# Routed experts ordered by token count, with 64 slots for the three smallest

## The chip, the cores and the metric

The kernel runs on one core of a Trainium2 chip. The metric is the device time of one execution in microseconds (us). A whole network of thirteen stages is one program; the change touches only the twelfth, the routed experts.

## The reference

The stage computes, for 256 tokens `xt` of width 1024, eight experts of width 3584 and two experts per token:

```
logits = (xt @ w_router).astype(jnp.float32)
top_v, top_i = lax.top_k(logits, TOP_K)
gates = jax.nn.softmax(top_v, axis=-1)
comb = jnp.sum(jax.nn.one_hot(top_i, N_EXPERTS) * gates[..., None], axis=1)
y = jnp.zeros_like(xt)
for e in range(N_EXPERTS):
    y = y + comb[:, e:e + 1] * swiglu(xt, wg[e], wu[e], wd[e])
```

`swiglu(x, wg, wu, wd)` is `(silu(x @ wg) * (x @ wu)) @ wd`. `y` is added to the residual, and a last RMS norm follows. On the inputs of this case the reference's router gives the experts 0 to 7 these numbers of tokens: 58, 42, 99, 63, 66, 73, 32, 79 (512 in all, two for each token).

## The kernel before, in words

All arithmetic is float32, made of fp32r products: each operand is split into a high part (a cast to fp32r on ACT, `whi`, L462) and a low part (the rest, a subtraction on DVE, `wlo`, L463), and a product is the sum of three matmuls: high by high, low by high, high by low. `mm` (L326) issues every matmul.

The weights of an expert come as 42 tiles of 1 MB, 128 x 2048 (`load`, L431; the DMA is issued by SP at L435). An expert is cut into `NG` = 7 groups of 512 of its 3584 inner columns. A group takes two tiles of `moe_g`, two of `moe_u` and two of `moe_d`; every tile is converted in two halves of 128 x 1024. The raw tiles go round 13 buffers (`raw`, `raw2`, `raw3`), the converted halves round `W_BUFS` = 4 pairs of buffers. SP can issue a tile as soon as DVE has made the second low half of the tile 13 places ahead of it.

`moe_round` (L1875) runs the experts 0 to 7 in their order:

- `places(ep)` builds, for a pair of experts, the 0/1 matrices `pm` (token by slot, 128 slots an expert) and gathers the input of each by matmuls into `mpg`, split into `gh` and `gl`.
- `up(x, g)` is a group's gate and up product: the standing operand is `gh` or `gl` (128 slots), the moving one 512 columns of weights: 8 steps of 128 input features by 3 matmuls for each of `eg` and `eu`, 48 in all. Then `ea` = silu(`eg`) * `eu` (ACT L1935, DVE L1936).
- `turn` transposes `ea` in four 128 x 128 pieces into `ept` and splits it into `eah`, `eal` (L477, L478).
- `down(x, g)` adds the group to the expert's sums `eacc`: 4 pieces by 2 halves of the output by 3 matmuls, 24.
- `back` scales the sums by the gates (`eyh`, `eyl`, L1968 and L1969), scatters them to tokens with the transposed `pm` (`esc`) and adds them to `x` (L1975).

A group's `down` comes one group late, and `turn` stands between the gate and the up product of the next group; a scheduler then sets the order on each engine. After expert 0's first group, `rest()` computes the gates and the largest count. A second round follows if an expert has more than 128 tokens (L1857, L1858); with the counts above it is skipped.

Of the kernel before, what the change touches and what calls it, by code (L numbers as in the profile page):

```python
# [230 lines left out]
# ---------------------------------------------------------------- device program  # L231
# [14 lines left out]
def hybrid_stack_kernel(ctx: ExitStack, tc: tile.TileContext, A, out, voff, coff, stages=STAGES):  # L246
# [5 lines left out]
    # the tiles of the stages; before the routed experts they make room for more raw weights  # L252
# [60 lines left out]
    def g4(name, shape, dt=F32):  # L313
        return pools["attn" if "attn" in pools else "work"].tile(list(shape), dt, tag="g4", name=name, bufs=6)
# [38 lines left out]
    # constants used as they come, and those that are converted first  # L353
# [66 lines left out]
    # ---- weights  # L420
# [3 lines left out]
    def behind(insts):  # L424
        # keep what is traced inside from being issued before these
# [40 lines left out]
    def load_last(name, i):  # L466
        # in smaller steps, as nothing follows that could hide them
# [64 lines left out]
    def square_step(q, acc, m):  # L532
        # squares of the outputs as they end, and sums of the earlier ones
# [15 lines left out]
    class OutProj:  # L549
# [15 lines left out]
        def feed(self, hi, lo):  # L565
# [13 lines left out]
            if self.k == self.nk:  # L579
                # the two that come last lie in different banks  # L580
# [6 lines left out]
    # ---- norms  # L587
# [28 lines left out]
    def col_sums(o, parts, first=True, last=True):  # L616
        # sums over the partitions, one token per row: o [P, 2]
# [6 lines left out]
    def spread(o, c, start=False):  # L624
        # a value per token, from rows to every partition of o [., T]
# [214 lines left out]
    def stack_hl(rows, n, dst):  # L840
        # rows: psum [n, W] -> dst [64, W] with the two parts on rows 0.. and 32..
# [3 lines left out]
    # ---- state-space mixer  # L845
    def ssm_stage():
# [20 lines left out]
        # time steps  # L867
# [25 lines left out]
        # minus the running sums; the first chunk's also as seen from the second  # L893
# [107 lines left out]
    # ---- cross attention  # L1001
# [126 lines left out]
    # ---- gated MLPs  # L1128
# [51 lines left out]
    # ---- convolution module  # L1180
    def cf_stage():
# [7 lines left out]
        def gate(w, o):  # L1189
            for b in range(2):  # L1190
# [7 lines left out]
                # twice the gated value; the halves are taken back below  # L1198
# [3 lines left out]
        def taps_pe(n):  # L1202
            # some of the taps, as products with diagonal matrices
# [102 lines left out]
    def head_scale(tiles, nq, gq, gk, st):  # L1306
        # unit-norm heads in place; both gains and the scale go on the keys
# [92 lines left out]
    def run_heads(n, score, turn, out, fill=(), a=LEAD):  # L1400
        # three steps per head, each behind the next head's earlier ones
# [16 lines left out]
    def ab_stage():  # L1418
# [3 lines left out]
        for part in range(2):  # L1422
# [5 lines left out]
            if part == 0:  # L1428
                # forget gate: negative log and its running sum
# [39 lines left out]
            def bias(hd):  # L1469
                def f(p):  # L1470
# [3 lines left out]
                    # the running sums are of the negated logs  # L1474
# [20 lines left out]
    def cd_stage():  # L1495
        h = begin()
        # differential half
# [62 lines left out]
        # sliding window half: query tile t holds heads t and t + 4  # L1560
# [65 lines left out]
    # ---- gated convolution and linear recurrence  # L1626
    def hybrid_stage(l):
# [6 lines left out]
        # the gate comes as half of one plus a tanh  # L1634
# [46 lines left out]
        # recurrence  # L1681
        ybs = []
        ss, la_, bb = [], [], []
        for i in range(4):
# [7 lines left out]
            # 1 - a^2 = -tanh(log a) (1 + a^2)  # L1692
# [8 lines left out]
        for s in ss:  # L1701
            # the square root takes the quarter that is due to the halved gate
# [37 lines left out]
    # ---- routed experts  # L1740
# [13 lines left out]
    def route_step(j):  # L1754
        # the mean square and the router, from x as it comes
# [24 lines left out]
    def moe_stage():  # L1780
# [37 lines left out]
        # slots count from one; a token that is not routed has zero  # L1818
# [5 lines left out]
        # the token-major copy of the normalised input  # L1824
# [8 lines left out]
        def rest():  # L1833
            # exp of (v - max) for the two, over their sum
# [11 lines left out]
            cnt = keep.tile([P, 8], F32, name="cnt")  # L1846
            dve.tensor_copy(cnt, pr[:, 0, 16:24])
            mc = keep.tile([P, 1], F32, name="mc")
            dve.tensor_reduce(mc, cnt, axis=AX.X, op=OP.max)
# [3 lines left out]

        ci = []
        moe_round(0, hth, htl, sel, comb, lambda: ci.append(rest()))
        # an expert with more than 128 tokens takes a second round
        most = nc.values_load(ci[0][0:1, 0:1], min_val=0, max_val=T)  # L1857
        with tc.If(most > P):  # L1858
            dve.tensor_scalar(sel, sel, -float(P), 0.0, op0=OP.add, op1=OP.add)
            moe_round(1, hth, htl, sel, comb)  # L1860

    def xtok(t, n):
        # x by tokens, in the place of x by features
# [10 lines left out]
    # sums of squares for the last norm  # L1874
    ss = keep.tile([P, 2, 2], F32, name="ss")  # L1875

    def moe_round(rnd, hth, htl, sel, comb, rest=None):
        def places(ep):
            pm = [t1("pm", (P, 2, P), F32R) for _ in range(2)]
            for t in range(2):  # L1880
                for u in range(2):
                    e = 2 * ep + u
                    dve.tensor_scalar(pm[t][:, u, :], iota, sel[:, t, e : e + 1], 0.0, op0=OP.is_equal, op1=OP.add)
            # gathered inputs of the pair
            gh = [g4("gh", (P, KD, P), F32R) for _ in range(2)]
            gl = [g4("gl", (P, KD, P), F32R) for _ in range(2)]
            pgs = []
            for k2 in range(4):
                pg = ps("mpg")
                for j in range(2):  # L1890
                    k = 2 * k2 + j
                    cs = slice((k % 4) * P, (k % 4 + 1) * P)
                    for t in range(2):
                        r = pm[t].rearrange("p u s -> p (u s)")
                        mm(pg[:, j, :], hth[2 * t + k // 4][:, cs], r, j == 0 and t == 0, False)
                        mm(pg[:, j, :], htl[2 * t + k // 4][:, cs], r, False, j == 1 and t == 1)
                pgs.append(pg)
            for u in range(2):
                for k2 in range(4):
                    ks = slice(2 * k2, 2 * k2 + 2)  # L1900
                    split(pgs[k2][:, :, u * P : (u + 1) * P], gh[u][:, ks, :], gl[u][:, ks, :])
            return [(2 * ep + u, gh[u], gl[u], [None, None], pm, u) for u in range(2)]

        def places_back(x):
            # slot-major places, and gates by slot
            e, pm, u = x[0], x[4], x[5]
            pb = t1("pb", (P, T), F32R)
            pt = ps("mpt2")
            for t in range(2):
                pe.transpose(pt[:, 0, t * P : (t + 1) * P], f32v(pm[t][:, u, :]), ident)  # L1910
            for t in range(2):
                mm(pt[:, 1, :8], f32v(pm[t][:, u, :]), comb[:, t, :], False, t == 1)
# [3 lines left out]
            x[3][:] = [pb, g]  # L1916

        def up(x, g, mid):
            e, gh, gl = x[:3]
            po = [wv("eg"), wv("eu")]  # L1920
            po = [a.rearrange("p a b -> p (a b)") for a in po]
            for i, src in enumerate(("moe_g", "moe_u")):
# [164 lines left out]
```

## Time and profile before

| | |
|---|---|
| three runs | 2750.71, 2752.17, 2752.65 us; median 2752.17 |
| profiled execution | 2753.1 us, which is also its span |
| busy: PE, DVE, ACT | 2697.2, 2201.6, 1728.4 us |
| stage of the experts | about 1717 to 2740 us of the span |

The span is from the first to the last instruction. An engine's busy time is the sum of its instructions; matmuls overlap their neighbours and their ends are modelled, so what a matmul costs is the step from one start to the next in the timeline.

### The profile page before, as it was taken

The numbers are of one execution on the slowest core, as the hardware profiler recorded it, in microseconds if no ns is written. First come the engines' busy times: TensorE is split into PE (matmuls) and PEld (weight loads), VectorE is DVE, ScalarE is ACT, GpSimd is POOL, SyncE is SP. The second block draws the span as 40 slices with busy tenths as digits, with TensorE's granted clock in tenths as the row PEclk, the third lists the DMA queues.
The fourth block names the chain that finished last, engine by engine and source line by source line (L and its number), as shares of the span: only waits on it lengthen the run. The fifth ranks groups of instructions, "written<-read, shape, count | busy, mean of one in ns | idle before, by whom it ended". The sixth has DMA issues, their size and how long they took to land. (4 is left out here: it accounts for less than half of the span.)

```text
span 2753.1 us, 44558 instructions
## 1 busy us (share of the span) xinstructions
PE 2697.2 (98%) x17440; PEld 2398.0 (87%) x17440; DVE 2201.6 (80%) x3344; ACT 1728.4 (63%) x2563; POOL 7.7 (0%) x76
## 2 busy tenths in 40 slices
PE   8999999999999999999999999999999999999997
PEld 8799999999889988888999999888887878787876
DVE  8787597798668776767875577999998888888887
ACT  6665465565656555555654455877777777777776
POOL 0000000000000000000000000000000000000000
PEclk9999999999999999999999999999999999999999
DMA  7145445433435543342655554999999999999993
GB/s 260 62 169 184 138 155 189 162 108 123 169 117 190 184 145 127 113 139 100 260 198 184 184 177 169 347 363 351 351 343 343 339 349 359 349 344 343 362 343 115
DMA packets 87259, 620.05 MB, mean 225 GB/s; under 512 B 9936, under 2 KB 10064, under 8 KB 12800
## 3 DMA queue, kind: packets, MB, share of 16 engines
q1 hardware_dynamic: 86608, 616.57, 62.3%
q8 instruction: 138, 2.26, 0.3%
q14 instruction: 81, 0.66, 0.1%
q10 hardware_dynamic: 432, 0.56, 0.1%
HBM read 616.04 MB, written 1.05 MB: 224 GB/s over the span
## 5 line engine op out<-in xcount | busy, mean ns | idle before, releaser
L463 DVE TENSOR_TENSOR wlo<-raw,whi 128x1024 fp32r<-128x1024 f32 (+1 forms) x1164 | 1390.1, 1219 | 343.3 <-ACT whi L462 335.5
L462 ACT CAST whi<-raw 128x1024 fp32r<-128x1024 f32 (+1 forms) x1164 | 1195.6, 1049 | 573.8 <-PE wv L326 296.4
L326 PE MATMUL wv<-hh,whi 128*128 128x256 f32 x2400 | 681.2, 285 | 14.7 <-ACT hh L661 13.4
L326 PE MATMUL wv<-hl,whi 128*128 128x256 f32 x2400 | 680.1, 284 | 0.1
L326 PE MATMUL wv<-hh,wlo 128*128 128x256 f32 x2400 | 677.0, 283 | 1.6 <-DVE wlo L463 1.5
L326 PEld LDWEIGHTS wv<-hh,whi 128*128 128x128 f32 x2400 | 456.4, 190 | 18.7 <-ACT hh L661 14.6
L326 PEld LDWEIGHTS wv<-hh,wlo 128*128 128x128 f32 x2400 | 455.7, 190 | 4.1 <-DVE wlo L463 3.2
L326 PEld LDWEIGHTS wv<-hl,whi 128*128 128x128 f32 x2400 | 456.9, 190 | 1.8 <-DVE hl L662 0.7
L326 PE MATMUL eg<-wlo,gh 128*128 128x512 f32 x448 | 178.5, 398 | 2.8 <-DVE wlo L463 2.8
L326 PE MATMUL eu<-whi,gh 128*128 128x512 f32 x448 | 179.5, 401 | 0.0
L326 PE MATMUL eu<-wlo,gh 128*128 128x512 f32 x448 | 177.7, 397 | 1.4 <-DVE wlo L463 1.3
L326 PE MATMUL eg<-whi,gh 128*128 128x512 f32 x448 | 178.3, 398 | 0.0
L326 PE MATMUL eg<-whi,gl 128*128 128x512 f32 x448 | 177.2, 395 | 0.0
L326 PE MATMUL eacc<-whi,eal 128*128 128x512 f32 x448 | 177.1, 395 | 0.0
L326 PE MATMUL eacc<-whi,eah 128*128 128x512 f32 x448 | 177.0, 395 | 0.0
L326 PE MATMUL eu<-whi,gl 128*128 128x512 f32 x448 | 177.0, 395 | 0.0
L326 PE MATMUL eacc<-wlo,eah 128*128 128x512 f32 x448 | 162.6, 400 | 0.0
L326 PE MATMUL acc<-fl,whi 128*128 128x256 f32 x576 | 161.7, 281 | 0.0
L326 PE MATMUL acc<-fh,wlo 128*128 128x256 f32 x576 | 161.1, 280 | 0.0
L326 PE MATMUL acc<-fh,whi 128*128 128x256 f32 x576 | 160.6, 279 | 0.0
L837 DVE SCALAR_TENSOR_TENSOR cv<-pad,vec,cv 128x256 f32<-128x256 f32 x288 | 124.8, 479 | 1.4 <-ACT cv L834 0.6
L326 PEld LDWEIGHTS acc<-fl,whi 128*128 128x128 f32 x576 | 108.2, 188 | 0.3 <-DVE fl L478 0.3
(539 smaller groups left out, 4302.6 us busy)
## 6 DMA issues: line engine op xcount, KB each, us to landing
raw<-moe_u SPq DMA_DIRECT2D x112, 1024.0 KB, 7.1
raw<-moe_g SPq DMA_DIRECT2D x112, 1024.0 KB, 7.1
raw<-moe_d SPq DMA_DIRECT2D x111, 1024.0 KB, 7.0
raw<-ffn_in SPq DMA_DIRECT2D x44, 1024.0 KB, 5.0
raw<-sw_in SPq DMA_DIRECT2D x28, 1024.0 KB, 5.0
raw<-ffn_out SPq DMA_DIRECT2D x22, 1024.0 KB, 5.0
raw<-hy_in SPq DMA_DIRECT2D x20, 1024.0 KB, 5.0
raw<-ssm_in SPq DMA_DIRECT2D x18, 1024.0 KB, 5.2
```

Of the source, the lines that this page charges most:

```text
L326: return pe.matmul(o, l, r, start=start, stop=stop, skip_group_check=True)
L462: act.copy(hi[:, cs], raw[:, cs])
L463: dve.tensor_sub(lo[:, cs], raw[:, cs], f32v(hi[:, cs]))
L837: dve.scalar_tensor_tensor(y, pad[:, j, 4 - s : 4 + T - s], taps[i], y, op0=OP.mult, op1=OP.add)
```

## The change

It does four things. (1) The experts run in an order that is made on the chip: `rest()` sorts them by count (expert 0 stays first), writes the order to `idx`, and permutes slots, gates and counts (`selp`, `combp`, `cp`). SP loads each position's expert number from `idx` into a register and addresses the weights by it. (2) `RANKS` says which rank runs at which position, and `CAPS` how many slots it has: the ranks 5, 6 and 7 have 64, at the positions 2, 5 and 7. (3) For these, one operand `gx` of 128 columns holds the high part in 64 and the low part in 64, so that a product takes two matmuls. Rows 0 to 63 and 64 to 127 of the result are summed later: `turn_small` copies `eg` and `eu` out, and its products with `twice` (two identities of 64, one above the other) turn and sum at once; silu and the product with `eu` come after that, on 128 x 4 x 64. `down_small` again takes two matmuls. (4) Gathering is by the groups `GROUPS` (one or two experts). The second round starts if a count is above its position's slots.

```
+RANKS = [0, 1, 5, 2, 3, 6, 4, 7]
+SMALL = 64
+CAPS = [P if r < 5 else SMALL for r in RANKS]
+GROUPS = [[0], [1, 2], [3, 4], [5, 6], [7]]
...
 rest():
+            dve.scalar_tensor_tensor(key, cnt, 8.0, iota8, op0=OP.mult, op1=OP.subtract)
+            dve.tensor_scalar(key[:, 0:1], key[:, 0:1], 8.0 * T + 16.0, 0.0, op0=OP.add, op1=OP.add)
+            dve.max(out=kv, in_=key)
+            dve.max_index(ki, kv, key)
+            for j, r in enumerate(RANKS):
+                dve.tensor_scalar(oh[:, j, :], iota8, kf[:, r : r + 1], 0.0, op0=OP.is_equal, op1=OP.add)
+                dve.tensor_copy(idx[:, j : j + 1], kf[:, r : r + 1])
+            for src, dst in ((sel[:, 0], selp[:, 0]), (sel[:, 1], selp[:, 1]), (cnt, cp), (comb[:, 0], combp[:, 0]), (comb[:, 1], combp[:, 1])):
+                dve.tensor_tensor(tmp, oh, bc2(src, 8), op=OP.mult)
+                dve.tensor_reduce(dst, tmp, axis=AX.X, op=OP.add)
+            for j, c in enumerate(CAPS):
+                dve.tensor_scalar(cp[:, j : j + 1], cp[:, j : j + 1], float(T - c), 0.0, op0=OP.add, op1=OP.add)
-        with tc.If(most > P):
+        with tc.If(most > T):
...
+        def fetch(raw, src, e, i, cs=slice(0, 2048)):
+                    regs[e] = nc.values_load(
+                        route["idx"][0:1, e : e + 1], engines=[mybir.EngineType.SP], min_val=0, max_val=NE - 1
+                w = A[src][bass.ds(regs[e], 1), i : i + 1, :, cs].rearrange("a b p n -> (a b p) n")
...
 up():
-                        mm(po[i], gh[:, k, :], whi[:, cs], k == 0, False)
-                        mm(po[i], gl[:, k, :], whi[:, cs], False, False)
-                        mm(po[i], gh[:, k, :], wlo[:, cs], False, k == KD - 1)
+                        for a in gx:
+                            mm(po[i], a[:, k, :], whi[:, cs], k == 0 and a is gx[0], False)
+                        mm(po[i], gx[0][:, k, :], wlo[:, cs], False, k == KD - 1)
+                if not big:
+                    s.append(t2("es", (P, 512)))
+                    act.copy(s[i], po[i])
...
+        def turn_small(s):
+            pt = ps("ept", (P, 2, 4, SMALL))
+            for i in range(2):
+                for j in range(4):
+                    mm(pt[:, i, j, :], s[i][:, j * P : (j + 1) * P], route["twice"], i == 0 and j == 0, i == 1 and j == 3)
+            act.activation(a, pt[:, 0], AF.Silu)
+            dve.tensor_mul(a, a, pt[:, 1])
+            split(a, ax[:, :, :SMALL], ax[:, :, SMALL:])
...
+        def down_small(x, g, a, acc):
+                    for n in range(2):
+                        mm(acc[n], a[:, 2 * c + j, :], whi[:, cs], g == 0 and c == 0 and j == 0, False)
+                        mm(acc[n], a[:, 2 * c + j, :], wlo[:, cs], False, g == NG - 1 and c == 1 and j == 1)
```

The order of the instructions moves with it. Three places matter. The first is ACT in one group: before the change, in an ordinary group (`eah` belongs to the group ahead).

```order
L462 CAST whi_23192<-raw2_23190 128x1024
L462 CAST whi_23196<-raw2_23190 128x1024
L1935 ACTIVATE ea_23234<-eg_23135 128x512
L462 CAST whi_23214<-raw2_23212 128x1024
L462 CAST whi_23218<-raw2_23212 128x1024
L462 CAST whi_23239<-raw2_23237 128x1024
L462 CAST whi_23243<-raw2_23237 128x1024
L462 CAST whi_23261<-raw2_23259 128x1024
L462 CAST whi_23265<-raw2_23259 128x1024
L477 CAST eah_23332<-ept_23327 128x512
```

And with the change, on the same engine, in a group of the expert at position 2, the first with 64 slots.

```order
L470 CAST whi_22945<-raw2_22943 128x1024
L470 CAST whi_22949<-raw2_22943 128x1024
L2014 COPY es_22926<-eg_22888 128x512
L485 CAST eax_22940<-eas_22937 128x4x64
L470 CAST whi_22963<-raw2_22961 128x1024
L470 CAST whi_22967<-raw2_22961 128x1024
L470 CAST whi_22983<-raw2_22981 128x1024
L470 CAST whi_22987<-raw2_22981 128x1024
L2014 COPY es_22979<-eu_22889 128x512
L470 CAST whi_23001<-raw2_22999 128x1024
L470 CAST whi_23005<-raw2_22999 128x1024
L2037 ACTIVATE eas_23075<-ept_23066 128x256
```

Two instructions of 128 x 512 become two copies and two smaller ones, and each copy stands between two pairs of conversions. The second place is DVE where the stage starts, before the change: `sel` has just been made.

```order
L1883 TENSOR_SCALAR pm_20022<-direct_79,sel_20004 128x128 x2
L1883 TENSOR_SCALAR pm_20023<-direct_79,sel_20004 128x128 x2
L1849 TENSOR_REDUCE mc_20190<-cnt_20188 128x1
L1851 CAST ci_20192<-mc_20190 128x1
L1831 SCALAR_TENSOR_TENSOR mtl_20015<-mpx_19938,mSt_19964,mth_20014 128x512
L463 TENSOR_TENSOR wlo_20089<-raw3_20086,whi_20088 128x1024
```

With the change the same stretch of DVE reads as follows; 16 more instructions for `oh` and `idx`, ten for the permutations and eight for `cp` stand among the next eight conversions.

```order
L1951 TENSOR_SCALAR pm_20024<-direct_79,sel_20004 128x128
L1951 TENSOR_SCALAR pm_20025<-direct_79,sel_20004 128x128
L1861 SCALAR_TENSOR_TENSOR key_20182<-cnt_20180,direct_79 128x8
L1862 TENSOR_SCALAR key_20182<-key_20182 128x1
L1864 MAX kv_20185<-key_20182 128x8
L1866 MAX_INDEX ki_20187<-kv_20185,key_20182 128x8
L1868 CAST kf_20189<-ki_20187 128x8
L1839 SCALAR_TENSOR_TENSOR mtl_20015<-mpx_19938,mSt_19964,mth_20014 128x512
```

The chain of the sort stands ahead of `mtl`, the low part of the tokens that the gathering needs. The third place is SP with the change, at expert 0's fourth group.

```order
L1927 DMA raw3_20529<-moe_d 128x2048
L1927 DMA raw2_20553<-moe_g 128x2048
L1920 TENSOR_LOAD idx_20191
L1920 ISA x2
L1920 TENSOR_LOAD idx_20191
L1920 ISA x2
L1920 TENSOR_LOAD idx_20191
L1920 ISA x2
L1927 DMA raw2_20575<-moe_g 128x2048
```

Three loads of the order, which wait for DVE's `idx`, now stand ahead of the other 25 tiles of expert 0; from position 1 on, one register instruction (`ISA`) stands ahead of each DMA.

## Rows read from the trace of the kernel before

**Rows 1.** The page: busy time of each engine; 40 slices of DMA and GB/s.

```profile
PE 2697.2 (98%) x17440; PEld 2398.0 (87%) x17440; DVE 2201.6 (80%) x3344; ACT 1728.4 (63%) x2563; POOL 7.7 (0%) x76
...
DMA  7145445433435543342655554999999999999993
GB/s 260 62 169 184 138 155 189 162 108 123 169 117 190 184 145 127 113 139 100 260 198 184 184 177 169 347 363 351 351 343 343 339 349 359 349 344 343 362 343 115
```

**Rows 2.** Windows: busy PE, PEld, DVE, ACT, POOL; granted clock, DMA share, GB/s.

```profile
1751.62:1768.85 17.23, 17.23 (x78) 13.92 (x77) 15.74 (x16) 13.51 (x15) 0.00 (x0) 1.00 0.97 361
1768.85:1786.07 17.22, 17.22 (x78) 13.91 (x77) 15.72 (x15) 13.51 (x15) 0.00 (x0) 1.00 0.96 361
```

**Rows 3.** Timeline of PE: start, length, instruction, count.

```profile
2105.14 0.40 PE L326 MATMUL eu<-wlo,gh 128*128 128x512 f32 x1
2105.37 0.40 PE L326 MATMUL eu<-whi,gh 128*128 128x512 f32 x1
2105.60 0.40 PE L326 MATMUL eu<-whi,gl 128*128 128x512 f32 x1
...
1721.68 3.17 PE L326 MATMUL mpx<-mdg,xT 128*128 128x128 f32 x26
```

**Rows 4.** Timeline of DVE behind expert 3, and behind expert 2 (last two).

```profile
2253.11 6.89 DVE L463 TENSOR_TENSOR wlo<-raw,whi 128x1024 fp32r<-128x1024 f32 x6
2259.92 0.68 DVE L1936 TENSOR_TENSOR ea<-ea,eu 128x512 f32<-128x512 f32 x1
2260.52 6.96 DVE L463 TENSOR_TENSOR wlo<-raw,whi 128x1024 fp32r<-128x1024 f32 x6
...
2118.63 0.75 DVE L1969 SCALAR_TENSOR_TENSOR eyl<-eacc,gsl,eyh 128x512 fp32r<-128x512 f32 x1
2119.29 2.47 DVE L1975 TENSOR_TENSOR xT<-xT,esc 128x512 f32<-128x512 f32 x4
```

**Rows 5.** Groups of the stage, 1700 to 2750 us: count, busy us, mean ns, idle.

```profile
L462 ACT CAST whi<-raw 128x1024 fp32r<-128x1024 f32 x673 | 684.0, 1052 | 97.8 <-PE eg L326 39.9 <-PE eacc L326 30.6 <-PE eu L326 21.2
L477 ACT CAST eah<-ept 128x512 fp32r<-128x512 f32 x56 | 32.7, 585 | 71.2 <-PE ept L1942 71.2
L478 DVE TENSOR_TENSOR gl<-mpg,gh 128x256 fp32r<-128x256 f32 x32 | 12.7, 419 | 3.7 <-ACT gh L477 3.4
L477 ACT CAST gh<-mpg 128x256 fp32r<-128x256 f32 x32 | 11.2, 379 | 14.3 <-PE mpg L326 13.8 <-DVE gl L478 0.4
L1883 DVE TENSOR_SCALAR pm<-direct,sel 128x128 fp32r<-128x128 f32 x16 | 4.1, 280 | 0.0
```

**Rows 6.** Timeline of ACT: the first `eyh` of experts 3 to 6.

```profile
2244.39 0.69 ACT L1968 ACTIVATE eyh<-eacc,gsl 128x512 fp32r<-128x512 f32 x1 [3.38 <-PE eacc L326]
...
2369.19 0.69 ACT L1968 ACTIVATE eyh<-eacc,gsl 128x512 fp32r<-128x512 f32 x1 [3.38 <-PE eacc L326]
...
2497.77 0.69 ACT L1968 ACTIVATE eyh<-eacc,gsl 128x512 fp32r<-128x512 f32 x1 [3.38 <-PE eacc L326]
...
2622.60 0.69 ACT L1968 ACTIVATE eyh<-eacc,gsl 128x512 fp32r<-128x512 f32 x1 [3.38 <-PE eacc L326]
```

**Rows 7.** SP's waits, tiles landed, SP's timeline, its one register load.

```profile
SPq L435 <- DVE wlo L463: 801.4, 309, 6.6
...
raw<-moe_g SPq DMA_DIRECT2D x109, 1024.0 KB, 7.1
...
1758.10 2.79 SPq L435 DMA_DIRECT2D raw<-moe_g  x2
...
L1857 SPq TENSOR_LOAD <-ci x1: 481/481/481, 1731.6 to 1731.6; - x1
```

**Rows 8.** Timeline of DVE at the stage's start, in `rest()`.

```profile
1740.58 0.17 DVE L1842 TENSOR_TENSOR gt<-gt,gs 128x4 f32<-128x4 f32 x1
1740.78 0.17 DVE L1843 TENSOR_TENSOR o<-o,gt 128x16 f32<-128x16 f32 x1
1740.87 0.17 DVE L1844 TENSOR_TENSOR o<-o,gt 128x16 f32<-128x16 f32 x1
```

**Rows 9.** Windows elsewhere: columns as in rows 2.

```profile
15.00:20.00 5.00, 4.34 (x35) 3.93 (x34) 4.12 (x7) 3.23 (x4) 0.00 (x0) 1.00 1.03 420
340.00:344.00 4.00, 1.51 (x11) 1.38 (x11) 2.05 (x11) 2.99 (x5) 0.00 (x0) 0.91 0.18 76
344.00:348.00 4.00, 2.35 (x9) 1.76 (x9) 3.02 (x8) 1.79 (x4) 0.00 (x0) 0.50 0.00 0
748.00:752.00 4.00, 2.67 (x15) 2.04 (x15) 2.73 (x11) 3.99 (x14) 0.00 (x0) 1.00 0.56 231
```

More of the change, by code (lines that the diff above doesn't have):

```diff
@@ L313, in g4 @@
     def g4(name, shape, dt=F32):
-        return pools["attn" if "attn" in pools else "work"].tile(list(shape), dt, tag="g4", name=name, bufs=6)
+        if "attn" in pools:
+            return pools["attn"].tile(list(shape), dt, tag="g4", name=name, bufs=6)
+        return pools["work"].tile(list(shape), dt, tag="g4", name=name, bufs=5)
     def sm(name, shape, dt=F32):
@@ L1852, in rest @@
             return ci
+        selp = keep.tile([P, 2, 8], F32, name="selp")
+        combp = keep.tile([P, 2, 8], F32, name="combp")
         ci = []
-        moe_round(0, hth, htl, sel, comb, lambda: ci.append(rest()))
-        most = nc.values_load(ci[0][0:1, 0:1], min_val=0, max_val=T)
-        with tc.If(most > P):
-            dve.tensor_scalar(sel, sel, -float(P), 0.0, op0=OP.add, op1=OP.add)
-            moe_round(1, hth, htl, sel, comb)
+        moe_round(0, hth, htl, sel, selp, combp, lambda: ci.append(rest()))
+        most = nc.values_load(ci[0][0:1, 0:1], min_val=0, max_val=2 * T)
+        with tc.If(most > T):
+            for j, c in enumerate(CAPS):
+                dve.tensor_scalar(selp[:, :, j : j + 1], selp[:, :, j : j + 1], -float(c), 0.0, op0=OP.add, op1=OP.add)
+            moe_round(1, hth, htl, selp, selp, combp)
     def xtok(t, n):
@@ L1961, in down @@
                         mm(acc[n], ah[:, f], wlo[:, cs], False, g == NG - 1 and c == 1 and j == 1)
+        def down_small(x, g, a, acc):
+            e = x[0]
+            for c in range(2):
+                end = e == NE - 1 and g == NG - 1 and c == 1
+                wt = (load_e_last if end else load_e)("moe_d", e, 2 * g + c)
+                for j in range(2):
+                    whi, wlo = wt[j]
+                    for n in range(2):
+                        cs = slice(n * 512, (n + 1) * 512)
+                        mm(acc[n], a[:, 2 * c + j, :], whi[:, cs], g == 0 and c == 0 and j == 0, False)
+                        mm(acc[n], a[:, 2 * c + j, :], wlo[:, cs], False, g == NG - 1 and c == 1 and j == 1)
         def back(x, acc):
-            pb, gs = x[3]
+            pb, gs = x[2]
             yh = [t2("eyh", (P, 512), F32R) for _ in range(2)]
@@ L1977, in back, with step_down, turned @@
                         act.activation(t2("fsq", (P, 512)), xtok(t, n), AF.Square, accum_out=ss[:, t, n : n + 1])
-        todo = places(0)
+        def step_down(late):
+            x, g, a, acc = late
+            if acc is None:
+                acc = [ps("eacc", (P, 512)) for _ in range(2)]
+            (down if x[4] else down_small)(x, g, a, acc)
+            if g == NG - 1:
+                back(x, acc)
+                acc = None
+            return acc
+        def turned():
+            if late:
+                late[2] = (turn if late[0][4] else turn_small)(late[2])
+        todo = places(GROUPS[0])
         late = None
@@ L1990, in moe_round @@
                 if late is not None:
-                    y, gg, aa, ac = late
-                    if ac is None:
-                        ac = [ps("eacc", (P, 512)) for _ in range(2)]
-                    down(y, gg, aa, ac)
-                    acc = ac
-                    if gg == NG - 1:
-                        back(y, ac)
-                        acc = None
+                    acc = step_down(late)
                 late = [x, g, a, acc]
-                if g == 3 and e % 2 and e < NE - 1:
-                    todo += places((e + 1) // 2)
+                if g == 3 and not todo and e < NE - 1:
+                    todo += places(next(q for q in GROUPS if q[0] == e + 1))
                 if g == 4:
                     places_back(x)
-        y, gg, aa, ac = late
-        down(y, gg, turn(aa), ac)
-        back(y, ac)
+        turned()
+        step_down(late)
     def final_stage():
```

98 lines of the change are left out of this document (72 added, 26 removed).

## The prediction, made before the change was run

> **What bounds the kernel now.** I read the page first, then windows of the experts' stage, then the timelines of single engines. The page [rows 1] shows PE busy for 98% of the span, but in the last 16 of 40 slices, the experts, the DMA engines are also at nine tenths and DVE close behind; busy shares don't say which of the three gives the pace. The windows do. Two neighbouring groups of an expert [rows 2] last 17.22 us each, with PE busy throughout, DVE for 15.7, ACT for 13.5. In the timeline of PE a matmul of 512 columns starts 0.233 us after the one before [rows 3], whatever its listed length: 72 of them are 16.8 us, and four transposes fill the rest. So PE bounds a group. ACT waits for it: the conversion's idle time, 97.8 us in all, ends on PE [rows 5]. SP waits 801 us for DVE to give buffers back [rows 7], so weights are ahead of their use.
>
> How far ahead sets what happens when PE gets faster. A tile has 17.22 / 6 = 2.87 us; its buffer is issued anew 13 tiles ahead, 37.3 us; 7.1 us go until it lands [rows 7], some 3 us in conversion. About 27 us are left, or nine landed tiles.
>
> **What the change removes.** In a group of 64 slots `up` goes from 48 matmuls to 32, `down` from 24 to 16. That is 24 x 0.233 = 5.6 us of PE in each of 3 x 7 = 21 groups, 118 us in all. It would be the gain if PE stayed the bound. The sum over the other engines says that it doesn't.
>
> **A small group, engine by engine.** PE: 48 x 0.233 = 11.2 us, plus eight products with `twice`, 128 x 64 columns in full float32. The trace has no such shape. The nearest row, `mpx` [rows 3], gives 3.17 / 26 = 0.12 us for an instruction of 128 columns and two instructions to a product: 0.24 us as upper end, 0.12 with half the columns as lower. So 0.9 to 1.9 us, and PE needs 12.1 to 13.1.
>
> DVE: twelve low parts, and two operations on 128 x 256. Six low parts back to back take 2259.92 - 2253.11 = 6.81 us [rows 4], 1.135 each, so 13.6; the two are priced by `gl`, 0.42 each [rows 5], 14.5 us together. ACT: twelve casts, two copies like `eah`, 0.585 each, two like `gh`, 0.38 [rows 5]: at its full lengths 14.6 us, less for overlapped ends. So **DVE becomes the bound**, PE idles a sixth of the time, and what ACT makes DVE wait comes on top. The listed order of ACT in a small group has a copy of `eg`, later of `eu`, between conversions, and each waits for the last matmul of its product. From the end of the low part that this product needs last: four matmuls 0.93, copy 0.59, the cast of `eax` 0.38 (first point only), the next conversion 1.05 [rows 5], three handoffs of some 0.05: 3.1 and 2.7 us. DVE has two low parts (2.3), and at the first point `eax`'s 0.42, in hand. It idles about 0.4 us each time. A small group takes 14.5 + 0.8 = **15.3 us** in place of 17.22.
>
> **Experts.** Before, the distance between the scaled sums of neighbouring experts is 124.8, 128.6, 124.8 us [rows 6]; 128.6 is one that also gathers the next pair. I take 124.6 and 4.0 for a gathering, hidden by nothing since PE is full.
> - A small expert: 7 x 15.3 = 107.1. The expert ahead of it adds its `back` on DVE: two `eyl` 1.5 and four `xT` 2.5 [rows 4], 4.1 with `gsl`; and ACT's two waiting `eyh` delay conversions, for which I take 1.0 by the bubbles above (nothing to 3.4, the wait in [rows 6], are the ends). Together 112.2.
> - The one at position 2 gathers the pair 3 and 4 too. On DVE: four `gl` as before 1.7, four of half the width and four `pm` by the row of `pm`, 0.28 each: 2.2 [rows 5]. So 116.1.
> - Sum: 340.5 against 3 x 124.6 = 373.8: 33.3 gained.
> - Gatherings on PE in large experts: three before, 12.0; now at positions 0, 4 and 6, the last with 128 columns a matmul (2 to 4 us, take 3): 11.0. One more gained.
>
> **At the start** DVE gets 5 instructions of the sort and 16 for `oh` and `idx`, ten for the permutations, eight for `cp`, before PE has work ahead. A dependent small step is 0.20 us, an independent one 0.09 [rows 8]: 15 x 0.20 + 24 x 0.09 = 5.2 us. It loses four `gl` at some 0.36, since expert 0 is gathered alone, and a little of `pm`. Net 3.6 us, taken as fully on the path (nothing and 5.2 are the ends). **At the end** the last conversion is followed by 4 matmuls instead of 6, and PE no longer lags: 1 us gained.
>
> SP's three loads of the order, 0.48 us each [rows 7], wait for `idx`, which stands behind seven conversions in DVE's order, about 8 us at 1.135 each and the small steps; 25 tiles of expert 0 stand behind them. Nine landed tiles cover that. If they were gone, a few us would show. A register step per DMA is nothing against 2.87 us per tile.
>
> Sum: 33.3 + 1.0 - 3.6 + 1.0 = 31.7 us off 2753.1, so 2721. The profiled execution is 0.9 us above the median of the runs: **2720 us**.
>
> **Do the weights keep up?** A small expert uses 42 tiles in 112 us, 2.67 us each. In [rows 2] the engines moved 361 GB/s, 2.90 us a tile of 1.049 MB, and that was demand, not a limit: [rows 9] has 420. At 361, a small expert draws 42 - 112 / 2.90 = 3.4 tiles from the nine, a large one adds 0.9. After position 2 that leaves 5.6, 7.5 ahead of position 5, 4.1 behind it, 5.0 ahead of position 7, and 1.6 at the end. So the stock lasts even then.
>
> The Trainium skill's page DMA: Bandwidth & Descriptors, section Where 436 GB/s comes from, puts a limit of about 358 GB/s from HBM for each core, and by it a group's six tiles would need 17.6 us, so that without a stock nothing could be gained. The trace disagrees in short windows (420 GB/s), and its longest stretch near full, the last slices of [rows 1], has 363 at most, which was demand.
>
> **The rivals.**
> - *DMA takes over.* For it: a share of 0.97 in [rows 2]. Against: SP waits for buffers, and the stock above. If the stock were nothing and 361 a limit, a small group would take 17.4 us, and only `back`, gatherings and the end remain: about 2746. With a stock used up halfway, 2733.
> - *ACT gives the pace.* If its copies and waits don't overlap, or the eight joining products hold up PE's queue, on which `eu`'s matmuls stand behind them, a group takes 16.2 us: 19 us more, 2739.
> - *Only DVE's work counts*: no bubbles, 14.5 us a group, 17 us less: 2703.
> - *Slower: the clock.* PE idles a sixth of the time in small groups. Where PE had done little, at 340 us (busy 1.5 of 4), the granted clock fell to 0.50, the lower of the two levels, 1.2 GHz [rows 9]. At twice the step a small group's PE takes 25 us, 21 x 8 = 168 us above now: about 2920. It decides from a share of a good third of half-rate time (12.6 x 1.37 = 17.2). Against: gaps of tenths of a us, and a clock of 1.00 where PE was busy 2.67 of 4 us [rows 9]. The skill's page TensorE: Matmul & The Clock Gate, section What's actually happening, says that the clock is halved after idleness and returns with activity; [rows 9] agree.
> - *Slower: a second round*, if the change doesn't do what it says: a count above 64 at a small position would repeat the stage, some 970 us. The counts sorted, expert 0 apart, are 99, 79, 73, 66, 63, 42, 32; the largest of the last three is 63. It takes 65. A register-addressed DMA that needed over 2.9 us to issue would also be slower, by what it exceeds.
>
> **How the numbers follow.** DVE's pace with its bubbles, 2710 to 2732: 0.65. Work alone, down to 2700: 0.10. ACT's pace: 0.10. DMA partly or wholly: 0.08, of it 0.02 at no change. Clock 0.04; a second round or slow DMAs 0.02; nothing for a reason not seen 0.01. The range, 2702 to 2741, has the bounds of a group's price (14.5 to 16.2) and of the start; it leaves out the lost stock, the clock and the rest. A measurement here tells 0.2%, 5.5 us, from no change: faster 0.91, same 0.03, slower 0.06.
>
> **What would show it.** Small experts lasting 110 to 118 us, with PE's clock at 1.00, DVE busy in over nine tenths of them and PE waiting for `wlo`; large experts as before; SP still waiting for DVE. It is wrong if `wlo` or `whi` waits for DMA in a small expert, if ACT's waits for `eg`, `eu` and `ept` exceed 2 us a group, if PE's steps there are above 0.233 us, or if the start costs over 6 us.

## The result, and the profile after

The changed kernel takes 2700.51 us (median of four, 2699.77 to 2704.30) against 2752.01 for the kernel before (four): a ratio of 0.9817, 95% interval 0.9803 to 0.9831. Faster, as forecast, but by 51.5 us instead of 32, and 1.5 us below the low end of the range.

The page of the changed kernel, the three lines that answer to [rows 1]:

```profile
PE 2630.7 (97%) x17220; PEld 2319.6 (86%) x17220; DVE 2189.1 (81%) x3385; ACT 1733.5 (64%) x2605; POOL 7.7 (0%) x76
...
DMA  7145345533535543343655555799999999999993
GB/s 265 63 158 200 134 153 192 179 110 107 175 109 184 188 145 125 126 156 102 250 189 188 187 178 184 259 340 355 364 373 393 351 347 340 359 408 369 341 377 154
```

PE loses 66.5 us of work; six slices rise to 364 to 408 GB/s: the three small experts. Windows of two neighbouring small groups (columns as in [rows 2]):

```profile
2401.76:2416.92 15.16, 14.62 (x65) 10.29 (x64) 14.47 (x16) 13.22 (x17) 0.00 (x0) 1.00 1.01 407
2416.92:2432.08 15.16, 14.61 (x65) 10.29 (x64) 14.47 (x16) 13.22 (x17) 0.00 (x0) 1.00 1.01 414
```

A group takes 15.16 us with DVE busy for 14.47, where the forecast had 15.3 and 14.5. Of the listed time of PE, 14.6, some 2 us are waiting inside matmuls: its 48 steps of 0.233 us and the 16 instructions of the turning, 0.091 us each, need 12.6. What a group takes beyond DVE's work are two gaps in the timeline of DVE, here one group:

```profile
2408.62 2.36 DVE L471 TENSOR_TENSOR wlo<-raw,whi 128x1024 fp32r<-128x1024 f32 x2 [0.36 <-ACT whi L470]
2410.90 0.41 DVE L2038 TENSOR_TENSOR eas<-eas,ept 128x256 f32<-128x256 f32 x1
2411.23 6.89 DVE L471 TENSOR_TENSOR wlo<-raw,whi 128x1024 fp32r<-128x1024 f32 x6
2418.04 0.42 DVE L486 TENSOR_TENSOR eax<-eas,eax 128x256 fp32r<-128x256 f32 x1
2418.79 4.63 DVE L471 TENSOR_TENSOR wlo<-raw,whi 128x1024 fp32r<-128x1024 f32 x4 [0.33 <-ACT whi L470]
```

They come where the forecast put them, 0.33 and 0.36 us instead of 0.4, and behind ACT's waits for PE at the copies, in the timeline of ACT:

```profile
2407.06 0.59 ACT L2014 COPY es<-eu 128x512 f32<-128x512 f32 x1 [0.61 <-PE eu L334]
2407.54 2.00 ACT L470 CAST whi<-raw 128x1024 fp32r<-128x1024 f32 x2
2409.76 0.38 ACT L2037 ACTIVATE eas<-ept 128x256 f32<-128x256 f32 x1 [0.23 <-PE ept L334]
2410.05 5.78 ACT L470 CAST whi<-raw 128x1024 fp32r<-128x1024 f32 x6
2416.92 0.59 ACT L2014 COPY es<-eg 128x512 f32<-128x512 f32 x1 [1.09 <-PE eg L334]
```

So the group went as forecast. (The three waits shown are 1.9 us a group, just under the 2 us that the prediction named as a sign of being wrong.) The surprise stands elsewhere. The stage's first DVE operation behind the mean square, `rvs`, and the first `eal`, the low part of expert 0's first group, in the timeline of DVE before the change, and then after it:

```profile
1719.80 0.16 DVE L611 TENSOR_SCALAR rvs<-ms 128x2 f32<-128x2 f32 x1 [3.25 <-PE ms L326]
...
1751.62 0.69 DVE L478 TENSOR_TENSOR eal<-ept,eah 128x512 fp32r<-128x512 f32 x1
```

```profile
1706.99 0.16 DVE L619 TENSOR_SCALAR rvs<-ms 128x2 f32<-128x2 f32 x1 [3.26 <-PE ms L334]
...
1743.78 0.68 DVE L486 TENSOR_TENSOR eal<-ept,eah 128x512 fp32r<-128x512 f32 x1
```

**12.8 us are won before the stage starts**, in eleven stages whose instructions and order are the same, but for one of 0.21 us on DVE that makes `twice`, at 17.8 us. From `rvs` to the first `eal` the change is 5.0 us slower (36.79 against 31.82), from there to the end 42.8 us faster (958.7 against 1001.5).

Two things differ ahead of the stage. The first is the clock. A window of the kernel before, and the same work after:

```profile
1282.00:1292.20 10.20, 10.20 (x41) 6.10 (x39) 5.07 (x23) 5.67 (x23) 0.00 (x0) 0.50 0.08 31
```

```profile
1276.45:1282.15 5.70, 5.70 (x41) 3.70 (x39) 5.02 (x23) 4.61 (x20) 0.00 (x0) 1.00 0.14 56
```

The profiled execution before ran 10.2 us at the lower level there, 1.2 GHz, the one after did not; what takes 10.2 us there takes 5.7 after, so that the distance of the two grows by 4.5 us at that place. The second is slow growth everywhere: 95 consecutive starts of `wv` products with 256 columns, in the timeline of PE. Second and last of them, before:

```profile
289.02 0.28 PE L326 MATMUL wv<-hl,whi 128*128 128x256 f32 x1
...
300.18 0.28 PE L326 MATMUL wv<-hh,wlo 128*128 128x256 f32 x1
```

And the same two after:

```profile
287.71 0.28 PE L334 MATMUL wv<-hl,whi 128*128 128x256 f32 x1
...
298.68 0.28 PE L334 MATMUL wv<-hh,wlo 128*128 128x256 f32 x1
```

94 steps take 11.16 us and 10.97: 118.7 ns and 116.7 a step. Over 6,300 such pairs of neighbours in each trace the means are 118.2 and 116.8: some 8.5 us of PE's time, against the 8.3 us that the clock leaves of the 12.8.

### The profile page after: what moved, and what is told of

It reads as the page before. It is cut to its first block, busy times and chain, and to the rows that moved or that the text cites. A ratio compares the mean times of both kernels' runs of the same rounds, so it can differ in the third digit from the quotient of the medians.

```text
span 2702.4 us, 44795 instructions
## 1 busy us (share of the span) xinstructions
PE 2630.7 (97%) x17220; PEld 2319.6 (86%) x17220; DVE 2189.1 (81%) x3385; ACT 1733.5 (64%) x2605; POOL 7.7 (0%) x76
## 5 line engine op out<-in xcount | busy, mean ns | idle before, releaser
L334 PEld LDWEIGHTS wv<-hh,whi 128*128 128x128 f32 x2400 | 456.5, 191 | 17.6 <-ACT hh L669 13.8
L334 PE MATMUL eu<-whi,gx 128*128 128x512 f32 x728 | 245.7, 400 | 0.0
L334 PE MATMUL eg<-whi,gx 128*128 128x512 f32 x728 | 245.0, 398 | 0.0
L334 PE MATMUL eg<-wlo,gx 128*128 128x512 f32 x448 | 184.8, 412 | 10.2 <-DVE wlo L471 9.9
L334 PE MATMUL eu<-wlo,gx 128*128 128x512 f32 x448 | 185.0, 413 | 5.0 <-DVE wlo L471 4.2
L334 PEld LDWEIGHTS eg<-whi,gx 128*128 128x128 f32 x728 | 137.0, 190 | 29.6 <-ACT whi L470 0.6
L334 PEld LDWEIGHTS eu<-whi,gx 128*128 128x128 f32 x728 | 135.3, 188 | 27.2 <-ACT whi L470 0.9
L334 PEld LDWEIGHTS eg<-wlo,gx 128*128 128x128 f32 x448 | 84.5, 189 | 51.8 <-DVE wlo L471 34.5
L845 DVE SCALAR_TENSOR_TENSOR cv<-pad,vec,cv 128x256 f32<-128x256 f32 x288 | 124.7, 478 | 1.4 <-ACT cv L842 0.6
L334 PEld LDWEIGHTS eu<-wlo,gx 128*128 128x128 f32 x448 | 84.1, 188 | 40.2 <-DVE wlo L471 23.3
L334 PE MATMUL eacc<-whi,eah 128*128 128x512 f32 x280 | 110.5, 395 | 0.0
L334 PE MATMUL eacc<-whi,eal 128*128 128x512 f32 x280 | 110.5, 395 | 0.0
```

What stands on the lines that cost most here:

```text
L334: return pe.matmul(o, l, r, start=start, stop=stop, skip_group_check=True)
L845: dve.scalar_tensor_tensor(y, pad[:, j, 4 - s : 4 + T - s], taps[i], y, op0=OP.mult, op1=OP.add)
```

## The experiments

Besides that one instruction, what the change does to those stages is in memory. `keep`, the pool of what lasts, grew by 384 bytes a partition (`twice`, `selp`, `combp`, `idx`, less `cnt`). The pool behind it, with all raw and converted weights, begins that much later: the first `whi` at byte 63040 of its partition instead of 62656, by the addresses in the two built programs.

**The place alone.** The kernel before, with 384 unused bytes (in the experts 16 instead of 20 small buffers make room):

```
+        gap = keep.tile([P, 96], F32, name="gap")
+        pool.memset(gap, 0.0)
```

> The kernel before, with nothing of the change but 384 unused bytes per partition ahead of the pool of raw and converted weights, so that this pool lies where the changed kernel has it. Theory A (12.8 us of the gain come ahead of the experts, from the place of the converted weights in SBUF): 2739 to 2746 us, the 256-column product step near 116.9 ns instead of 118.2, and the first DVE rvs near 1707 to 1713 us instead of 1719.8. Rival B (those 12.8 us belong to the run or the chip, not to the program): 2751 to 2753 us, step 118.2 ns.

Measured: 2744.24 us against 2751.09, ratio 0.9974 (0.9963 to 0.9986); `rvs` at 1708.02. The same two matmuls:

```profile
288.16 0.28 PE L326 MATMUL wv<-hl,whi 128*128 128x256 f32 x1
...
299.13 0.28 PE L326 MATMUL wv<-hh,wlo 128*128 128x256 f32 x1
```

10.97 us again. The place of a pool is worth 6.9 us, 0.26%, with not one instruction of the experts changed. In its profile 11.8 us are won by `rvs`, since this execution too lacks the stretch at 1282 us. And the other way round, the change with its tables in the experts' own pool:

```
-            tw = route["twice"] = keep.tile([P, SMALL], F32, name="twice")
+            tw = route["twice"] = early("twice", [P, SMALL])
...
-        selp = keep.tile([P, 2, 8], F32, name="selp")
-        combp = keep.tile([P, 2, 8], F32, name="combp")
+        selp = early("selp", [P, 2, 8])
+        combp = early("combp", [P, 2, 8])
```

> The changed kernel, with its three new kept tables (384 bytes) moved into the experts' own pool, so that the pool of weights lies where the kernel before has it. Theory A: 2707 to 2713 us, first rvs back near 1714 to 1720 us, step 118.2 ns. Rival B: 2699 to 2702 us, step 116.9 ns.

Measured: 2710.38 us (0.9848, 0.9835 to 0.9862), mean step 118.5 ns. Theory A stands in both directions.

**The small slots alone.** The change with 128 slots everywhere (`CAPS = [P for r in RANKS]`, six buffers for `gx`, 16 small buffers):

> The changed kernel with 128 slots for all eight experts: sorting, loads by register and the new gatherings stay, the 64-slot path is gone. If the three small experts are worth 14 us each, and the rest of the change costs some 5 us at the start of the stage while 12.8 us are won ahead of it: 2742 to 2748 us. Rival (the order by count and the single gatherings bring a good part of the gain in the experts): under 2738 us. Rival (the 64-slot path brings all of it, and the 12.8 us belong to the run): over 2751 us.

Measured: 2751.07 us, 0.9997 (0.9988 to 1.0006). The first expectation was too low by 3 us, and the last one right in number, but half of its reason is wrong: the 12.8 us don't belong to the run. The four profiled spans give a chain: before 2753.1, moved pool 2742.1, all large 2751.2, the change 2702.4. From the moved pool to all large: 0.4 us ahead of `rvs`, 5.0 from `rvs` to `eal`, 3.7 behind it, where the positions 0 and 7 are now gathered alone, so that the stage pays for five gatherings instead of four (position 6, which now gathers for 7, takes 128.8 us instead of 124.9). From all large to the change: 48.8 us, of which 47.3 behind `eal` and 1.5 ahead of `rvs`, where the two programs do the same.

**The start.** First the order of the experts written into the program, with no sort and no register:

```
+ORDER = [0, 2, 3, 7, 5, 1, 4, 6]
...
-                w = A[src][bass.ds(regs[e], 1), i : i + 1, :, cs].rearrange("a b p n -> (a b p) n")
+            w = A[src][ORDER[e], i][:, cs]
```

> The changed kernel with the order of the experts written into the program (the order that these inputs give): no sorting on VectorE, no number of an expert in a register, plain addresses in all loads of expert weights; the 64-slot path stays. If the sorting behind the second product of expert 0 costs the 5 us by which the stage's start became longer: 2695 to 2697.5 us, and from the first rvs to the first eal 32 us instead of 36.8. Rival (the start is longer by the two single gatherings or by the halved clock there): 2699 to 2702 us. Rival (loads by register hold up SP's queue all along): under 2692 us.

Measured: 2705.08 us; `rvs` to `eal` 36.57. The sort costs 0.2 us, not 5, and loads by register cost nothing that can be seen. Windows of the change show what the start loses:

```profile
1708.10:1711.50 3.40, 3.40 (x17) 3.15 (x16) 2.30 (x19) 0.15 (x1) 0.00 (x0) 0.50 0.96 349
1711.50:1718.30 6.80, 4.82 (x44) 4.46 (x43) 5.76 (x19) 6.59 (x11) 0.00 (x0) 1.00 0.85 328
1718.30:1725.10 6.80, 6.80 (x23) 5.93 (x24) 6.08 (x18) 3.79 (x8) 0.00 (x0) 0.50 0.71 251
```

10.2 us at half the clock are worth 5.1. Was that chance? The change once more:

> The changed kernel itself, once more beside the kernel before. If the two short halvings of the granted clock at the start of the experts' stage (1708 to 1711 and 1718 to 1725 us in its first profile) came by the chance of that execution: most executions at 2699 to 2702 us with a mean granted clock of 0.993, single ones near 2704 us with 0.991. If they belong to the program: all near 2704 us, as in the kernel with the order written in (2705.1 us at 0.990 to 0.991).

Measured: 2705.34 us, five executions from 2701.35 (mean granted clock 0.993) to 2705.89 (0.990), ratio 0.9823 (0.9809 to 0.9836). By the mean clock some executions of the change have these stretches, and others hardly any. Then two kernels whose first gathering is 256 columns wide as before: the fixed order in four pairs, `GROUPS = [[0, 1], [2, 3], [4, 5], [6, 7]]`, and the change itself with expert 0's places twice, the second half unused:

> The kernel with the order of the experts written in, gathered in four pairs as in the kernel before instead of one, three pairs, one. Against the fixed order in groups of one, two, two, two, one (2705.1 us): theory (five gatherings cost the 5 us that the all-large kernel lost against the moved kernel before inside the experts): 2699 to 2702 us. Rival (the number of gatherings costs nothing, the halved clock at the start is all): 2704 to 2706 us, or with the halvings gone 2700 to 2701 us and the steps within the experts as they were.

> The changed kernel with the first gathering 256 columns wide, expert 0's places twice, the second half unused, so that TensorE does at the start of the experts' stage what it did before the change. Theory (the halved clock at the start comes with the products of 128 columns, and is the whole loss there): no stretch at 0.5 between 1690 and 2690 us, first rvs to first eal 32 to 33 us instead of 36.8, 2699 to 2701 us, each execution at a mean of 0.992 to 0.993. Rival (the start is longer since one expert alone is gathered, or by the place of the clock's windows): 35 us or more, 2703 to 2706 us.

```
-            w = len(es) * P
+            w = T if es[0] == 0 else len(es) * P
...
+                if es[0] == 0:
+                    dve.tensor_copy(pm[t][:, P:], f32v(pm[t][:, :P]))
```

Measured: 2698.60 and 2700.16 us, clock 0.992 or 0.993 in all eight executions, `rvs` to `eal` 31.88 and 31.77. Windows of the wide one:

```profile
1707.10:1710.50 3.40, 3.40 (x29) 3.26 (x30) 2.86 (x21) 1.45 (x3) 0.00 (x0) 1.00 0.98 330
...
1717.30:1724.10 6.80, 6.80 (x33) 5.58 (x32) 6.77 (x8) 5.69 (x9) 0.00 (x0) 1.00 0.81 267
```

With the clock up the start costs nothing, sort and all. Of the profiles here, the six kernels that gather 256 columns first have no stretch at 0.50 in the start; all that gather 128 have one or two. But the earlier one begins 1.1 us behind `rvs`, some 6 us ahead of the first gathering, where PE's order is the same in both. So how the width comes to matter stays open. The pairs take 1.6 us less: they have one gathering less, and no sort.

**What bounds a small group.** The product `eas * ept` left out (the output lacks that factor for the small experts):

```
-            dve.tensor_mul(a, a, pt[:, 1])
```

> The changed kernel without the product of the silu with the up half in the 64-slot groups (0.4 us of VectorE and one hand-over in each of 21 groups; the output lacks that factor for these experts). Theory (VectorE's work and its two short waits set the 15.15 us of such a group): 14.65 to 14.8 us in the steady groups, 2691 to 2695 us. Rival A (the weights' transfers at 411 GB/s set it): 15.15 us, 2699 to 2702 us. Rival B (the chain through ScalarE's copies sets it): 15.1 us or more, 2698 us or more.

Measured: 15.04 us a group, 2703.64 us. DVE has 0.33 us less to do and gets 0.11 back. Its timeline:

```profile
2403.11 0.42 DVE L486 TENSOR_TENSOR eax<-eas,eax 128x256 fp32r<-128x256 f32 x1
2403.86 4.63 DVE L471 TENSOR_TENSOR wlo<-raw,whi 128x1024 fp32r<-128x1024 f32 x4 [0.33 <-ACT whi L470]
2408.85 8.26 DVE L471 TENSOR_TENSOR wlo<-raw,whi 128x1024 fp32r<-128x1024 f32 x7 [0.35 <-ACT whi L470]
```

Where the product stood, the next low part now waits inside its group of seven (8.26 us against 7 x 1.135 + 0.08 = 8.03): ACT's chain, which waits at each copy, is only 0.1 us behind DVE. The time is rival B's: nothing is gained on the change. So the copies were put off by one weight tile, to when their products have ended:

```
-                    act.copy(s[i], po[i])
+                    held.append([2, s[i], po[i]])
...
+            while held and held[0][0] == 0:
+                with behind([raws["cast"]]):
+                    act.copy(*held.pop(0)[1:])
```

> The changed kernel with ScalarE's copies es of the 64-slot groups issued one weight tile later (two casts each), when their products have ended. Theory (VectorE's two waits of 0.4 us a group are ScalarE standing at es for TensorE, 1.0 and 0.6 us, before the next cast): steady groups 14.5 to 14.9 us instead of 15.15, 2688 to 2698 us with the change itself at 2700 to 2705. Rival A (the four buffers of converted halves make ScalarE wait for TensorE anyhow, at the cast instead of the copy): 15.0 to 15.15 us. Rival B (the transfers, 6.29 MB a group, end at 411 to 418 GB/s): 15.05 us or more.

Measured: 14.93 us a group, 2705.56 us. Timeline of ACT, and then of DVE:

```profile
2407.35 0.38 ACT L2043 ACTIVATE eas<-ept 128x256 f32<-128x256 f32 x1 [1.84 <-PE ept L334]
```

```profile
2407.77 0.42 DVE L2044 TENSOR_TENSOR eas<-eas,ept 128x256 f32<-128x256 f32 x1
2408.71 2.36 DVE L471 TENSOR_TENSOR wlo<-raw,whi 128x1024 fp32r<-128x1024 f32 x2 [0.52 <-ACT whi L470]
2410.99 0.42 DVE L486 TENSOR_TENSOR eax<-eas,eax 128x256 fp32r<-128x256 f32 x1
2411.32 11.44 DVE L471 TENSOR_TENSOR wlo<-raw,whi 128x1024 fp32r<-128x1024 f32 x10
```

Both waits at the copies are gone; one came back, at the joined product `ept`, which now comes later. The steady groups gain 0.22 us each, but the kernel isn't faster than the change. From the first `ea` of position 1 to that of position 3 this profile takes 230.5 us instead of 232.3, and from 4 to 6 238.8 instead of 239.5. Behind the first `ea` of position 6 it loses 4.8: there it has a stretch of 6.8 us at 0.50, at 2677 us near the end of the last small expert, that the change doesn't have. That stretch is worth 3.4 at most; where the rest goes was not followed up. With a fifth pair of buffers in the experts as well, for one raw buffer less:

> As the kernel with the late copies, with a fifth pair of buffers for converted halves in the experts, in the place of one of 13 buffers for raw weights. Theory (the loop of four buffers between ScalarE, VectorE and TensorE sets what VectorE still waits): VectorE without waits, 14.45 to 14.6 us a group, 2685 to 2692 us, at 432 to 435 GB/s. Rival (the transfers set the pace): 15.0 us or more a group at 411 to 420 GB/s, 2698 us or more. Rival (VectorE's waits were the late copies alone): no gain over the kernel with the late copies.

Measured: 14.93 us again, 2707.25 us. The loop of four buffers is not what DVE waits for. The transfers aren't either: [rows 2] had 361 GB/s, the groups above 407 and 414, and SP still waits for DVE to give buffers back, 36.6 of the 45 us from 2395 to 2440 us of the change. Its waits there:

```profile
SPq L1927 <- DVE wlo L471: 24.0, 12, 2.5
SPq L1927 <- DVE eas L2038: 6.5, 3, 2.5
SPq L1927 <- DVE eax L486: 6.1, 3, 2.0
```

The Trainium skill's page DMA: Bandwidth & Descriptors, section Where 436 GB/s comes from, has about 358 GB/s from HBM as a core's limit; these windows pass it by some 15%. The Trainium skill's page Perfetto Trace Analysis, section Roofline, has that figure as the share of a core whose neighbour is active too, and some 120% of it as the ceiling of one alone; with that the windows agree.

**Which place.** Six more places of the pool, by the size of `gap`, with the tables in the experts' pool as above:

> The changed kernel with the pool of weights moved by 64 bytes downwards, so that every tile of converted weights begins at a multiple of 512 bytes of its partition (62976 for the first; 63040 in the change, 62656 in the kernel before). Theory (the remainder of the address by 256 or 512 sets the step of the 256-column products, and none is best): step under 116.9 ns, 2690 to 2699 us. Rival (only the distance to the other operands' addresses matters, with no such rule): step between 116.5 and 118.5 ns, 2699 to 2711 us.

> The changed kernel with the pool of weights at 62848 instead of 63040 bytes (384 past a multiple of 512; the kernel before has 192, the change 64, the slow one 0). If the step of the 256-column products falls with the distance from a multiple of 512: under 116.9 ns, 2690 to 2700 us. If 64 past a multiple is a lucky place: 118 to 120 ns, 2707 to 2725 us.

> The changed kernel with the pool of weights at 63104 bytes, 128 past a multiple of 512. If the time falls from 0 to 64 and rises again by 192 smoothly: 2700 to 2707 us. If only odd multiples of 64 are good (64 and 192 against 0 and 384): 2715 us or more.

> The same at 62720 bytes, 256 past a multiple of 512 (a multiple of 256). If multiples of 256 are bad: 2720 us or more, step of the 256-column products 119 ns or more. If only multiples of 512 are: 2710 us or less.

> The same at 62784 bytes, 320 past a multiple of 512, which is 64 past a multiple of 256 as in the change. With a rule by 256: 2700 to 2706 us, step near 116.9 ns. With one by 512, or by the distance to other tiles: another time, 2708 us or more.

> The same at 62912 bytes, 448 past a multiple of 512, which is 192 past a multiple of 256 as in the kernel before. With a rule by 256: 2708 to 2712 us, step near 118.3 ns. With one by the distance to a multiple of 512 on either side: as at 64, 2700 to 2706 us.

| first `whi`, bytes past a multiple of 256 | 0 | 64 | 128 | 192 |
|---|---|---|---|---|
| us, past 512: the same | 2725.00 | 2700.51, 2705.34 | 2717.25 | 2710.38 |
| us, past 512: 256 more | 2725.73 | 2704.80 | 2722.73 | 2710.45 |
| mean step of `wv<-hh,whi`, ns | 120.0, 120.1 | 116.8, 116.9 | 118.3, 118.4 | 118.5, 118.5 |

(2722.73 is one execution, at a clock of 0.989.) The rule is by 256 bytes: each place and the one 256 further agree in the step within 0.2 ns. The guess that a multiple of 512 is best was wrong by 25 us: the change came out at the best of these eight places, by chance. The two matmuls at a multiple of 256:

```profile
290.67 0.28 PE L334 MATMUL wv<-hl,whi 128*128 128x256 f32 x1
...
301.94 0.28 PE L334 MATMUL wv<-hh,wlo 128*128 128x256 f32 x1
```

94 steps in 11.27 us, 119.9 ns. Two places between, with the wide first gathering:

> The changed kernel with the first gathering 256 columns wide and the pool of weights at 63072 bytes, 96 past a multiple of 256, where the normalised inputs hh of the same products also lie. If the time falls towards the hh tiles' own place: under 2698 us, step of the 256-column products under 116.8 ns. If it runs between the neighbours 64 and 128: 2705 to 2712 us, step 117 to 118.5 ns.

> The same with the pool at 62752 bytes, 32 past a multiple of 256. If it runs between the neighbours 0 and 64: 2708 to 2716 us, step 117 to 120 ns. If the best place lies below 64: under 2698 us, step under 116.8 ns.

Measured: 2718.36 us at 96 (step 119.8), **2695.43 us at 32** (2694.55 to 2697.83; 0.9798, 0.9781 to 0.9814). At 96 neither expectation holds. The kernel at 32 is the fastest that still sorts on the chip: its time is that of the second expectation and its step, 117.5 and above the change's, that of the first. What it has besides is 952.9 us from `eal` to the end, 5.5 less than the wide one at 64. The `ea` of two neighbouring groups of position 0, in the timeline of ACT at 64, and then at 32:

```profile
1738.72 0.59 ACT L2020 ACTIVATE ea<-eg 128x512 f32<-128x512 f32 x1
...
1755.95 0.59 ACT L2020 ACTIVATE ea<-eg 128x512 f32<-128x512 f32 x1
```

```profile
1741.00 0.59 ACT L2022 ACTIVATE ea<-eg 128x512 f32<-128x512 f32 x1
...
1758.05 0.59 ACT L2022 ACTIVATE ea<-eg 128x512 f32<-128x512 f32 x1
```

A large group takes 17.05 us instead of 17.23. The mean step of the 512-column products into `eg` and `eu` is 230 ns instead of 233, that of those into `eacc` 233 in both. So the place acts in the experts as well, where PE is the bound: 5.1 of the 5.5 us lie in the five large experts.

## Why the prediction was wrong

The medians close: 2751.1 for before, 6.9 less for the place, 43.8 less behind `eal` (the moved kernel before 1002.2, the wide first gathering 958.4) give 2700.4; measured 2700.16. Against the forecast of 2720, point by point:

- **The step that failed first is one that the prediction never wrote down**: that stages with the same instructions keep their time. Its sum starts at 2753.1, counts the stage alone and so puts the rest at nothing, without a reason. The place of the pool gave 6.9 us there.
- **The start**: "Net 3.6 us, taken as fully on the path". Zero, its lower end. DVE's small steps were hidden; what the profile of the change loses there, 5.0 us, is the clock, which the prediction looked for in the small groups only.
- **A small group, 15.3 us**: right, and right in its parts: 15.16, DVE 14.47, two gaps of 0.33 and 0.36.
- **PE's share**: `ept` was bounded at 0.12 to 0.24 us a product; its instruction steps by 0.091 us, two to a product: 0.18.
- **A small expert, 112.2 us**: 112.70 at position 5 from its first copy to the next expert's `ea`, in the timeline of ACT:

```profile
2335.57 0.59 ACT L2014 COPY es<-eg 128x512 f32<-128x512 f32 x1 [1.01 <-PE eg L334]
...
2448.27 0.60 ACT L2018 ACTIVATE ea<-eg 128x512 f32<-128x512 f32 x1 [1.82 <-PE eg L334]
```

- **Position 2, 116.1 us**: 112.61. Its gathering was priced at 3.9 us; the fixed pairs, which don't gather there, take 109.45, so it costs 3.2. The rest is its first step, 18.0 us where position 5 has 21.0.
- **What the sum lacked** are the passages into and out of a small expert, which it puts at nothing: it prices every group of a small expert at DVE's pace and every large one as before. From all large to the change, the positions 1, 4 and 6, each ahead of a small one, become 3.6, 1.9 and 2.6 us shorter, from their first `ea` to the small expert's first copy: PE is still the bound there, and the first small group's gate product ends eight matmuls, 1.9 us, earlier. Position 3 becomes 1.7 longer. Position 4 with all large, and after the change (it ends at the copy at 2335.57 above):

```profile
2227.11 0.60 ACT L2018 ACTIVATE ea<-eg 128x512 f32<-128x512 f32 x1 [1.98 <-PE eg L334]
...
2355.77 0.60 ACT L2018 ACTIVATE ea<-eg 128x512 f32<-128x512 f32 x1 [1.98 <-PE eg L334]
```

```profile
2208.76 0.60 ACT L2018 ACTIVATE ea<-eg 128x512 f32<-128x512 f32 x1 [1.98 <-PE eg L334]
```

- **Gatherings**: "One more gained", with a gathering at position 2 priced in the small expert: 2.9 us of cost by the two terms together. All large against the moved kernel: 3.7.
- **The end**: position 7, from its first copy to `eyh`, takes 111.1 us instead of 124.7 when it is large, 13.6 where 12.4 and 1.0 had been given. Right.
- **The rivals.** DMA falls (407 to 424 GB/s in small groups, and no conversion of the stage waits for a transfer); ACT as the pace falls (15.16, not 16.2), though it is only 0.1 us behind; the clock falls in the small groups (1.00 throughout); no second round. "Only DVE's work counts", 2703, had the nearest time and the wrong reason: the gaps are there.
- **The range**, 2702 to 2741, names the bounds of a group's price and of the start, but its low end isn't their sum: 14.5 us a group and nothing at the start are 17 and 3.6 us less than 2720, 2699. The measured time lies above that sum, but not for its reasons: a group took 15.16 us, not 14.5.

So the mechanism of the change in a group was right. From all large to the change, positions 2, 5 and 7 (the last with the end) save 14.9, 12.2 and 13.8 us, where 12.5, 12.4 and 13.4 were forecast. The miss of 19.5 us is 6.9 for the place, 3.6 at the start and 8.2 in the experts (6.3 net in the neighbours, 2.4 at position 2, 0.4 at 7, less 0.2 at 5 and 0.8 in the gatherings); the last 0.8 us aren't placed. All three are on one side.

## What to carry to other kernels

A change that makes a kept table larger moves every pool behind it: compare the addresses of the tiles that feed the products before a sum is made, and test the old code at the new place before the new code gets the credit. When a stage moves from one engine's pace to another's, its first group and the group ahead of it still run at the old one, so price the passage apart. A gap that ends on another engine's copy goes elsewhere when the copy is moved, and work taken from the engine that sets the pace is won only as far as the next chain stands behind it: of 0.33 us less on DVE, 0.11 came back.

## What the runs showed that was not expected

- A product's step depends on where its converted weights lie: 116.8 ns at 64 bytes past a multiple of 256, 120.1 at 0, for the same instruction; 25 us over the kernel. Which conflict makes it, and with what, was not found. The 512-column products into `eg` and `eu` show it too, less: 230 ns a step at 32, 233 at 64 and 192.
- One core moved 407 and 414 GB/s in neighbouring windows of 15 us.
- Stretches of 3.4 to 10.2 us at half the clock show in single profiles, at 1282 us before and in the start of the experts after; by the mean granted clock (0.990 to 0.993) they come and go between executions of one program.
